# Hybrid decoder layer, feed-forward part: two norms placed later, accumulators folded by two row blocks, one subtraction on two engines, half of the last gamma products on GpSimd

## The chip, the cores and the metric

One core of a Trainium2 chip runs the whole layer as one program. The metric is the device time of one execution in microseconds (us); lower is better. TensorE is called PE here, VectorE DVE, ScalarE ACT, GpSimd POOL; SP is the engine whose queue issues nearly all transfers.

## What is computed

The layer has three parallel token mixers, a post-norm, and a squared-ReLU feed-forward with a second post-norm. The mixers are not touched by the change. What matters here, with S = 1024 tokens, a model width of 1024, a hidden width of 4096 and everything in float32:

```python
    h = layer_norm(alpha * h + mix, ln1_g, ln1_b)
    ff = jnp.square(jax.nn.relu(h @ w_up)) @ w_down
    h = layer_norm(alpha * h + ff, ln2_g, ln2_b)

def layer_norm(x, g, b):
    mu = jnp.mean(x, axis=-1, keepdims=True)
    xc = x - mu
    var = jnp.mean(xc * xc, axis=-1, keepdims=True)
    return xc * lax.rsqrt(var + LN_EPS) * g + b
```

## The kernel before, in words

**Arithmetic.** Every float32 operand of a product is split into a high part (a copy to the type fp32r, on ACT, line 76) and a low part (the difference, on DVE or POOL, line 77); a product is three PE passes, high by high, high by low, low by high (line 61). So each weight tile `W` and each operand tile `BT` or `MG` reaches PE by a transfer, a copy on ACT and a subtraction on POOL or DVE. Most of the feed-forward is computed by a block scheme with seven products in place of eight: sums and differences of 512-wide blocks are multiplied, and the seven results are added up.

**First norm.** The last part of the mixers ends with the projection `w_o`, done in two halves of 512 tokens. For the second half four row blocks n = 0 to 3 are normalised by `layer_norm` (two of them with ACT and POOL sharing the work, two, n = 2 and 3, on DVE alone but for one small power on POOL, line 1181), stored to `d_h1`, and a `flip_h1` for each is put on a list: it transposes the block and builds the split operands `xs[3]` to `xs[7]` from it on DVE, ACT and POOL, in a buffer of the ring of four that the weights use too (`W`).

**Up projection.** The first EARLY = 10 of 16 pairs are begun by `first_two`, which needs only the operands that are there already; flips 0 to 3 are taken from the list after the pairs 1, 3, 5 and 7. `c11` is the sum of two products (line 296), followed by the activation on ACT and a store. Then the 16 pairs are finished.

**Down projection.** `down(c, j, w)` is product j (1 to 7) of step c (0 to 6): four row blocks b of 512 columns go to PSUM (8 banks in rings of 3, 3 and 2, tiles `pz`, `ps`, `pt`) and are added on DVE to the SBUF accumulator `pa[j]`, 128 x 4 x 512. `pa[1]` and `pa[2]` share a tile of the ring `X`, `pa[4]` and `pa[0]` the other; `pa[5]` and `pa[3]` share a tile of the ring `O`, `pa[7]` and `pa[6]` the other. In step 0 the accumulators 2, 3 and 5 start from the rows of `h`, loaded from `d_h1`; `pa[3] -= pa[5]` (line 1058, on POOL) must come before product 5 is added to `pa[5]` (line 1070, DVE). In step 6 the products come in the order 1, 7, 3, 6, 2, 5, 4, and between them whole accumulators of 128 x 2048 are folded into each other on DVE (line 296): 6 += 1, 7 += 6, 6 += 5, 5 += 7, 4 += 7, 3 += 6, 2 += 1. After that `pa[2]` and `pa[3]` hold the two column halves of rows 0 to 3, `pa[4]` and `pa[5]` those of rows 4 to 7.

**Last rows.** The last two pairs are multiplied directly: `last_rows` computes for row blocks 4 and 5 together, then 6, 7, 0, 1, 2, 3 one by one, two PSUM tiles of 512 columns, adds each to its accumulator on DVE, takes the statistics (line 1147), and `norm_rows` does the second norm: mean and variance (1205, 1206) on DVE, a power on POOL (1207), four small operations on DVE (1208 to 1211), the scaling of each half on ACT (1213), times gamma on DVE (1214), plus beta on POOL (1215; on DVE for the last row), and the store of each half.

**Who sets the order.** A scheduler turns the program into one instruction list per engine, from the order in which it is written and an estimate of what each engine does; on the chip each engine takes its own list strictly in order, and waits where an operand isn't there. So where code stands decides only in part where its instructions stand.

Of the kernel before, what the change touches and what calls it, by code (L numbers as in the profile page):

```python
# [12 lines left out]
ALU = mybir.AluOpType  # L13
# [12 lines left out]
LN_EPS = 1e-5  # L26
# [9 lines left out]
def hybrid_layer(ctx: ExitStack, tc: tile.TileContext, a: dict, out: bass.AP):  # L36
    nc = tc.nc
# [16 lines left out]
    def const(name, shape, dt=F32):  # L54
        return sb.tile(shape, dt, tag="c_" + name, name=name, bufs=1)
# [78 lines left out]
    mhalf = const("mhalf", [P, 8])  # L134
# [15 lines left out]
    d_h1 = dr.tile([8, P, 1024], F32, name="d_h1")  # L150
# [144 lines left out]
    def add(o, a_, b_, op=ALU.add):  # L295
        nc.vector.tensor_tensor(out=o, in0=a_, in1=b_, op=op)  # L296
# [462 lines left out]
    for hf in range(NH):  # L759
# [42 lines left out]
        v = keep()  # L802
# [7 lines left out]
        for h in range(8):  # L810
# [9 lines left out]
            if h % 2 == 0 and h < 6:  # L820
                v = zv(h // 2 + 1)()
# [32 lines left out]
        lng, lnb = ln_consts(nc, st, a["ln1_g"], a["ln1_b"])  # L854
        bn = [sb.tile([P, 4, 6], F32, tag="bn", name=nm("bn"), bufs=8) for _ in range(4)]
# [21 lines left out]
        def flip_h1(n, rb, hf=hf):  # L877
# [33 lines left out]
            nc.vector.tensor_tensor(out=b21, in0=b21, in1=b22, op=ALU.subtract)  # L911
            part(4, b21, nc.vector)

        if hf == 1:
            xs[1] = (nx[0][:, 0:4], nx[1][:, 0:4])
            xs[2] = (nx[0][:, 4:8], nx[1][:, 4:8])
            operand_tiles()
        for n in range(4):
            rb = r[n // 2][:, n % 2, :]
            layer_norm(nc, small, rb, bn[n][:, 0:2, :], lng, lnb, 4.0 * LN_EPS, mhalf, None, hf == 0 or n < 2)  # L920
            nc.sync.dma_start(d_h1[4 * hf + n], rb)
            deferred.append(lambda n=n, rb=rb: flip_h1(n, rb))

    def psum(k):
# [6 lines left out]
    def first_two(i):  # L931
        w1 = halves(load_raw(a["w_up"][2 * i]), nc.gpsimd)
        o = pt("z")
        prod(o, w1, 0, 1)
        s1 = snap(o)
        nc.sync.dma_start(d_p1[i], s1)
        d = pt("s")
        prod(d, w1, 1, 2)
        c11 = st("G", [P, TH])
        add(c11, d, s1)  # L940
        act2(c11)
        nc.sync.dma_start(d_ff[i, 1], c11)

    for i in range(EARLY):
        first_two(i)
        if i % 2 and i < 8:
            deferred.pop(0)()

# [68 lines left out]
    pa = {}  # L1017

    def acc_pair(tag, i, j):
        t = st(tag, [P, 2, 4, TH])  # L1020
        pa[i], pa[j] = t[:, 0], t[:, 1]
# [3 lines left out]
    def rows_h1(j, h, f_):  # L1025
        nc.sync.dma_start(pa[j], d_h1v[:, 4 * h:4 * h + 4, f_, :])
# [22 lines left out]
    def down(c, j, wsrc):  # L1049
        f, w = operands(c, j, wsrc)  # L1050
        if c == 0 and j == 1:
            acc_pair("X", 1, 2)
            rows_h1(2, 0, 0)
            acc_pair("O", 5, 3)
            rows_h1(5, 1, 1)
            rows_h1(3, 0, 1)
            acc_pair("O", 7, 6)
            nc.gpsimd.tensor_tensor(out=pa[3], in0=pa[3], in1=pa[5], op=ALU.subtract)
        if c == 0 and j == 4:
            acc_pair("X", 4, 0)  # L1060
            rows_h1(0, 1, 0)
        for b in range(4):
            o = psum(turn[0] + b)
            bs = slice(b * P, (b + 1) * P)
            for jj in range(2):
                mm(o, f[:, 0, jj, bs], w[:, 0, jj, :], jj == 0, False)
                mm(o, f[:, 0, jj, bs], w[:, 1, jj, :], False, False)
                mm(o, f[:, 1, jj, bs], w[:, 0, jj, :], False, jj == 1)
            if c == 0 and j in (2, 3, 5):
                nc.vector.scalar_tensor_tensor(out=pa[j][:, b, :], in0=pa[j][:, b, :], scalar=ALPHA, in1=o,  # L1070
                                               op0=ALU.mult, op1=ALU.add)
            elif c == 0:
                nc.scalar.copy(pa[j][:, b, :], o)
            else:
                add(pa[j][:, b, :], pa[j][:, b, :], o)

    for c in range(NC - 1):
        m0, m1 = wd_raw(c)
        b11, b12, b21, b22 = m0[:, :, 0], m0[:, :, 1], m1[:, :, 0], m1[:, :, 1]
        down(c, 1, b11)  # L1080
        add(b11, b12, b11, ALU.subtract)
        if c < NC - 2:
            down(c, 2, b21)
            down(c, 5, b11)
            add(b12, b22, b12, ALU.subtract)
            down(c, 3, b22)
            down(c, 7, b12)
            add(b22, b22, b11, ALU.subtract)
            down(c, 6, b22)
            add(b21, b21, b22, ALU.subtract)  # L1090
            down(c, 4, b21)
            if c == 1:
                nc.vector.scalar_tensor_tensor(out=pa[4], in0=pa[0], scalar=ALPHA, in1=pa[4], op0=ALU.mult,
                                               op1=ALU.add)
            continue
        add(b12, b22, b12, ALU.subtract)
        down(c, 7, b12)
        down(c, 3, b22)
        add(b22, b22, b11, ALU.subtract)
        down(c, 6, b22)  # L1100
        add(pa[6], pa[6], pa[1])
        add(pa[7], pa[7], pa[6])
        down(c, 2, b21)
        add(b21, b21, b22, ALU.subtract)
        down(c, 5, b11)
        add(pa[6], pa[6], pa[5])
        add(pa[5], pa[5], pa[7])
        down(c, 4, b21)
        add(pa[4], pa[4], pa[7])

    lng, lnb = ln_consts(nc, st, a["ln2_g"], a["ln2_b"])
    ffs, wds = [], []
    for j in range(2):
        for m in range(2):
            i = NFF - 2 + j
# [4 lines left out]
            split(f[:, 0], f[:, 1], raw.rearrange("p h t -> p (h t)"), nc.gpsimd)  # L1120
            ffs.append(f)
            wds.append(weight(a["w_down"][2 * i + m], nc.vector if m else nc.gpsimd))
    add(pa[3], pa[3], pa[6])
    add(pa[2], pa[2], pa[1])
    def last_rows(bs):
        oo = {}
        for b in bs:
# [22 lines left out]
                      lambda cs, v, b=b: nc.sync.dma_start(outv[b][:, cs], v), b == 3)  # L1150

    last_rows((4, 5))
    for b in (6, 7, 0, 1, 2, 3):
        last_rows((b,))


def rsqrt(nc, small, v, scale, eps, mhalf, n):
# [10 lines left out]
def ln_consts(nc, st, g, b):  # L1168
    res = []
    for v in (g, b):  # L1170
        t = st("S", [P, D])
        nc.scalar.dma_start(t, bass.AP(tensor=v.tensor, offset=v.offset, ap=[[0, P], [1, D]]))
        res.append(t)
    return res


def layer_norm(nc, small, x, bn, g, b, eps, mhalf, store=None, spread=False):
    mv, e, y, z = small(2), small(1), small(1), small(1)
    nc.vector.bn_aggr(out=mv, in_=bn)
    nc.vector.tensor_scalar(out=e, in0=mv[:, 1:2], scalar1=eps, scalar2=None, op0=ALU.add)  # L1180
    nc.gpsimd.tensor_tensor(out=y, in0=e, in1=mhalf[:, :1], op=ALU.pow)
    if isinstance(x, list):
        parts = x
        for v, cs in parts:
            nc.vector.scalar_tensor_tensor(out=v, in0=v, scalar=mv[:, 0:1], in1=g[:, cs], op0=ALU.subtract,
                                           op1=ALU.mult)
    else:
        parts = [(x[:, c * 512:(c + 1) * 512], slice(c * 512, (c + 1) * 512)) for c in range(2)]
        nc.vector.scalar_tensor_tensor(out=x, in0=x, scalar=mv[:, 0:1], in1=g, op0=ALU.subtract, op1=ALU.mult)
    nc.vector.scalar_tensor_tensor(out=z, in0=y, scalar=e, in1=y, op0=ALU.mult, op1=ALU.mult)  # L1190
    nc.vector.tensor_scalar(out=z, in0=z, scalar1=-0.5, scalar2=1.5, op0=ALU.mult, op1=ALU.add)
    nc.vector.tensor_tensor(out=y, in0=y, in1=z, op=ALU.mult)
    for v, cs in parts:
        if spread:
            nc.scalar.activation(v, v, AF.Copy, scale=y)
            nc.gpsimd.tensor_tensor(out=v, in0=v, in1=b[:, cs], op=ALU.add)
        else:
            nc.vector.scalar_tensor_tensor(out=v, in0=v, scalar=y, in1=b[:, cs], op0=ALU.mult, op1=ALU.add)
        if store:
            store(cs, v)  # L1200


def norm_rows(nc, small, parts, bn, g, b, eps, mhalf, store, last):
    mv, e, y, z, nb = small(2), small(1), small(1), small(1), small(1)
    nc.vector.bn_aggr(out=mv, in_=bn)
    nc.vector.tensor_scalar(out=e, in0=mv[:, 1:2], scalar1=eps, scalar2=None, op0=ALU.add)
    nc.gpsimd.tensor_tensor(out=y, in0=e, in1=mhalf[:, :1], op=ALU.pow)
    nc.vector.scalar_tensor_tensor(out=z, in0=y, scalar=e, in1=y, op0=ALU.mult, op1=ALU.mult)
    nc.vector.tensor_scalar(out=z, in0=z, scalar1=-0.5, scalar2=1.5, op0=ALU.mult, op1=ALU.add)
    nc.vector.tensor_tensor(out=y, in0=y, in1=z, op=ALU.mult)  # L1210
    nc.vector.scalar_tensor_tensor(out=nb, in0=mv[:, 0:1], scalar=-1.0, in1=y, op0=ALU.mult, op1=ALU.mult)
    for v, cs in parts:
        nc.scalar.activation(v, v, AF.Identity, scale=y, bias=nb)
        nc.vector.tensor_tensor(out=v, in0=v, in1=g[:, cs], op=ALU.mult)  # L1214
        (nc.vector if last else nc.gpsimd).tensor_tensor(out=v, in0=v, in1=b[:, cs], op=ALU.add)  # L1215
        store(cs, v)

# [77 lines left out]
```

## Time and profile before

| what | us |
|---|---|
| median of 3 runs (lowest, highest) | 2167.03 (2166.65, 2169.42) |
| the profiled execution, its own time | 2166.51 |
| its span, first to last instruction | 2164.7 |
| PE busy | 2054.9 (95%) |
| DVE busy | 1252.5 (58%) |
| POOL busy | 959.3 (44%) |
| ACT busy | 837.7 (39%) |

All sums of the prediction are made against the profiled execution. Its time stands 1.8 us above its span, and 0.5 us below the median. The busy shares are means over the whole program; the stages that the change touches are the first begun pairs (from about 1484 us on), the first down step (from about 1807 us) and the end (from about 2078 us).

### The profile page before, as it was taken

How to read it: one execution, taken by the hardware profiler on the slowest of the kernel's cores; microseconds unless marked ns; L12 is line 12 of the kernel's file. 1: busy time of each engine (PE TensorE's matmuls, PEld its weight loads, DVE VectorE, ACT ScalarE, POOL GpSimd, SP SyncE). 2: the span in 40 equal slices, each digit the busy share in tenths (PEclk: the TensorE clock that was granted, in tenths of full speed). 3: DMA queues.
4: the chain of work that ended last, by engine and by line, in shares of the span. 5: the costliest groups of instructions: out<-in, count | busy, mean ns of one | idle time of the engine just before them, and what ended most of it. 6: DMA issues, size and time to landing. Idle time of an engine off the chain costs nothing. (4 is left out here: it accounts for less than half of the span.)

```text
span 2164.7 us, 26923 instructions
## 1 busy us (share of the span) xinstructions
PE 2054.9 (95%) x10050; PEld 1688.5 (78%) x10050; DVE 1252.5 (58%) x2092; ACT 837.7 (39%) x1480; POOL 959.3 (44%) x478
## 2 busy tenths in 40 slices
PE   8969998999999999999999999999899999999996
PEld 8747776777787898877778889887678887788875
DVE  5643276566536346256753624626566656598898
ACT  5423222344335233335433614333544454433322
POOL 2556665421222522751122242274533334777674
PEclk9989999999999999999999999999999999999998
DMA  8653432422233323544123332354657547744322
GB/s 281 215 161 127 155 121 93 145 89 69 60 102 110 124 84 117 177 145 136 59 69 103 102 123 84 121 187 144 199 186 228 182 145 240 275 136 154 116 88 78
DMA packets 125762, 299.30 MB, mean 138 GB/s; under 512 B 11408, under 2 KB 24896, under 8 KB 125632
## 3 DMA queue, kind: packets, MB, share of 16 engines
q1 hardware_dynamic: 124736, 294.42, 41.7%
q10 hardware_dynamic: 896, 3.16, 0.5%
q8 instruction: 79, 1.29, 0.3%
q14 instruction: 51, 0.42, 0.1%
HBM read 232.51 MB, written 65.03 MB: 137 GB/s over the span
## 5 line engine op out<-in xcount | busy, mean ns | idle before, releaser
L77 POOL TENSOR_TENSOR W<-R,W 128x1024 fp32r<-128x1024 f32 x205 | 497.0, 2426 | 879.3 <-ACT W L76 835.1
L61 PE MATMUL pz<-X,W 128*128 128x512 f32 x2016 | 491.9, 398 | 30.5 <-ACT W L76 11.3
L76 ACT CAST W<-R 128x1024 fp32r<-128x1024 f32 (+1 forms) x287 | 293.8, 1024 | 469.5 <-PE pz L61 226.1
L61 PEld LDWEIGHTS pz<-X,W 128*128 128x128 f32 x2016 | 377.7, 191 | 114.4 <-POOL W L77 12.9
L61 PE MATMUL pz<-O,W 128*128 128x512 f32 x1152 | 267.1, 391 | 0.0
L61 PEld LDWEIGHTS pz<-O,W 128*128 128x128 f32 x1152 | 214.9, 188 | 46.2 <-issue 1.5
L61 PE MATMUL pt<-O,W 128*128 128x512 f32 x768 | 188.0, 393 | 2.3 <-DVE T L296 2.3
L61 PEld LDWEIGHTS pt<-O,W 128*128 128x128 f32 x768 | 142.3, 188 | 39.5 <-DVE T L296 10.3
L77 DVE TENSOR_TENSOR W<-R,W 128x1024 fp32r<-128x1024 f32 (+1 forms) x84 | 100.5, 1197 | 75.3 <-ACT W L76 74.9
L61 PE MATMUL pz<-BT,W 128*128 128x512 f32 x384 | 102.1, 419 | 24.8 <-DVE G L315 9.7
L61 PEld LDWEIGHTS pz<-BT,W 128*128 128x128 f32 x384 | 76.4, 203 | 47.6 <-issue 12.7
L61 PE MATMUL ps<-W,BT 128*128 128x512 f32 x360 | 98.4, 391 | 5.3 <-DVE X L296 3.3
L61 PE MATMUL pz<-W,BT 128*128 128x512 f32 x354 | 96.3, 390 | 0.4 <-DVE X L1070 0.4
L61 PE MATMUL pz<-W,X 128*128 128x256 f32 x768 | 95.8, 284 | 0.0
L77 POOL TENSOR_TENSOR BT<-R,BT 128x1024 fp32r<-128x1024 f32 x27 | 72.1, 2671 | 51.4 <-ACT BT L76 51.4
L61 PE MATMUL ps<-X,W 128*128 128x512 f32 x384 | 93.0, 391 | 1.6 <-DVE G L296 1.6
L61 PEld LDWEIGHTS pz<-W,X 128*128 128x128 f32 x768 | 93.1, 192 | 0.0
L61 PE MATMUL ps<-T,W 128*128 128x512 f32 x384 | 92.2, 389 | 0.0
L61 PEld LDWEIGHTS ps<-X,W 128*128 128x128 f32 x384 | 72.6, 189 | 17.5 <-DVE G L296 2.3
L341 POOL TENSOR_TENSOR R<-R,R 128x512 f32<-128x512 f32 x48 | 64.3, 1340 | 48.8 <-DMA R<-in_w_gate_dram 31.1
L61 PEld LDWEIGHTS ps<-T,W 128*128 128x128 f32 x384 | 72.1, 188 | 15.0
L77 POOL TENSOR_TENSOR MG<-R,MG 128x1024 fp32r<-128x1024 f32 (+1 forms) x30 | 79.5, 2651 | 9.0 <-ACT MG L76 9.0
(277 smaller groups left out, 3454.9 us busy)
## 6 DMA issues: line engine op xcount, KB each, us to landing
R<-d_ff SPq DMA_DIRECT2D x49, 512.0 KB, 3.6
R<-in_w_b_dram SPq DMA_DIRECT2D x48, 512.0 KB, 3.5
R<-in_w_up_dram SPq DMA_DIRECT2D x42, 512.0 KB, 4.1
R<-in_w_gate_dram SPq DMA_DIRECT2D x40, 512.0 KB, 3.6
d_ff<-T SPq DMA_DIRECT2D x56, 256.0 KB, 2.8
d_z<-T SPq DMA_DIRECT2D x52, 256.0 KB, 2.0
G<-d_z SPq DMA_DIRECT2D x48, 256.0 KB, 2.8
d_ff<-S SPq DMA_DIRECT2D x48, 256.0 KB, 2.3
```

The source lines that it names most:

```text
L61: nc.tensor.matmul(o, lhsT=l, rhs=r, start=start, stop=stop, skip_group_check=more)
L76: (hi_copy or nc.scalar.copy)(hi, src)
L77: (lo_eng or nc.gpsimd).tensor_tensor(out=lo, in0=src, in1=f32(hi), op=ALU.subtract)
L341: nc.gpsimd.tensor_tensor(out=o, in0=a_, in1=b_, op=op)
```

## The change

It has four parts. In the first norm, the norms of row blocks 2 and 3 of the second half are written after the begun pairs 2 and 4 instead of ahead of pair 0. In the first down step, the subtraction `pa[3] -= pa[5]` is done half on DVE and half on POOL, and stands ahead of the allocation of the next pair of accumulators. In the last down step the folds are done for two row blocks at a time (128 x 1024), 14 operations for 7, some of them written later. In the second norm, the product with gamma of the second half of every row but the last is on POOL, where the additions of beta are already.

```diff
+        norms = []
         for n in range(4):
             rb = r[n // 2][:, n % 2, :]
-            layer_norm(nc, small, rb, bn[n][:, 0:2, :], lng, lnb, 4.0 * LN_EPS, mhalf, None, hf == 0 or n < 2)
-            nc.sync.dma_start(d_h1[4 * hf + n], rb)
+
+            def norm(n=n, rb=rb, hf=hf, bn=bn[n], gb=(lng, lnb)):
+                layer_norm(nc, small, rb, bn[:, 0:2, :], *gb, 4.0 * LN_EPS, mhalf, None, hf == 0 or n < 2)
+                nc.sync.dma_start(d_h1[4 * hf + n], rb)
+
+            if hf == 0 or n < 2:
+                norm()
+            else:
+                norms.append(norm)
             deferred.append(lambda n=n, rb=rb: flip_h1(n, rb))
...
     for i in range(EARLY):
         first_two(i)
+        if i in (2, 4):
+            norms.pop(0)()
         if i % 2 and i < 8:
             deferred.pop(0)()
...
             rows_h1(3, 0, 1)
+            for e, eng in enumerate((nc.vector, nc.gpsimd)):
+                bb = slice(2 * e, 2 * e + 2)
+                eng.tensor_tensor(out=pa[3][:, bb, :], in0=pa[3][:, bb, :], in1=pa[5][:, bb, :], op=ALU.subtract)
             acc_pair("O", 7, 6)
-            nc.gpsimd.tensor_tensor(out=pa[3], in0=pa[3], in1=pa[5], op=ALU.subtract)
...
+    def merge(h, *terms):
+        bb = slice(2 * h, 2 * h + 2)
+        for i, j in terms:
+            add(pa[i][:, bb, :], pa[i][:, bb, :], pa[j][:, bb, :])
...
         down(c, 6, b22)
-        add(pa[6], pa[6], pa[1])
-        add(pa[7], pa[7], pa[6])
         down(c, 2, b21)
         add(b21, b21, b22, ALU.subtract)
+        merge(0, (6, 1), (7, 6))
         down(c, 5, b11)
-        add(pa[6], pa[6], pa[5])
-        add(pa[5], pa[5], pa[7])
+        merge(1, (6, 1), (7, 6))
         down(c, 4, b21)
-        add(pa[4], pa[4], pa[7])
+        merge(0, (6, 5), (5, 7), (4, 7))
...
-    add(pa[3], pa[3], pa[6])
-    add(pa[2], pa[2], pa[1])
...
     last_rows((4, 5))
+    merge(1, (6, 5), (5, 7), (4, 7))
     for b in (6, 7, 0, 1, 2, 3):
         last_rows((b,))
+        if b >= 6:
+            merge(b - 6, (3, 6), (2, 1))
...
         nc.scalar.activation(v, v, AF.Identity, scale=y, bias=nb)
-        nc.vector.tensor_tensor(out=v, in0=v, in1=g[:, cs], op=ALU.mult)
+        (nc.vector if last or cs.start == 0 else nc.gpsimd).tensor_tensor(out=v, in0=v, in1=g[:, cs], op=ALU.mult)
         (nc.vector if last else nc.gpsimd).tensor_tensor(out=v, in0=v, in1=b[:, cs], op=ALU.add)
```

Three places of the instruction lists. The lines of `norm_rows` are 17 higher in the changed kernel: 1224 is the power, 1225 to 1228 are the four small operations, 1230 is ACT's scaling, 1231 gamma, 1232 beta. The tiles named `sm` hold one number per row.

First, DVE at the norms of row blocks 2 and 3 (T_11218 holds both, S the constants; G<-ps,G is c11 of pair 0, and W_11639 or W_11611 the buffer of flip 0). Before:

```order
L1190 SCALAR_TENSOR_TENSOR sm_11536<-sm_11535,sm_11534 128x1
L1179 BN_AGGR sm_11547<-bn_11228 128x2
L296 TENSOR_TENSOR G_11595<-ps_11582,G_11579 128x512
L1191 TENSOR_SCALAR sm_11536<-sm_11536 128x1
L1180 TENSOR_SCALAR sm_11548<-sm_11547 128x1
L1189 SCALAR_TENSOR_TENSOR T_11218<-T_11218,sm_11547,S_11221 128x1024
...
L1198 SCALAR_TENSOR_TENSOR T_11218<-T_11218,sm_11549,S_11223 128x512 x2
L296 TENSOR_TENSOR G_11634<-ps_11621,G_11618 128x512
L905 TENSOR_TENSOR W_11639<-W_11639 128x512
```

With the change:

```order
L296 TENSOR_TENSOR G_11567<-ps_11554,G_11551 128x512
L1207 SCALAR_TENSOR_TENSOR sm_11681<-sm_11680,sm_11679 128x1
L1196 BN_AGGR sm_11798<-bn_11228 128x2
L1208 TENSOR_SCALAR sm_11681<-sm_11681 128x1
L1197 TENSOR_SCALAR sm_11799<-sm_11798 128x1
L1206 SCALAR_TENSOR_TENSOR T_11218<-T_11218,sm_11798,S_11221 128x1024
...
L1215 SCALAR_TENSOR_TENSOR T_11218<-T_11218,sm_11800,S_11223 128x512 x2
L296 TENSOR_TENSOR G_11606<-ps_11593,G_11590 128x512
L905 TENSOR_TENSOR W_11611<-W_11611 128x512
```

c11 of pair 0 has moved up by two small rows; both norms still stand ahead of the first row of flip 0 (L905). In SP's list, the store of row block 2 now stands behind two stores of begun pairs, and that of block 3 behind four.

Second, POOL in the last rows, from the power of row 6 to the power of row 7 and a little further. Before:

```order
L1207 TENSOR_TENSOR sm_16210<-sm_16209,mhalf 128x1
L1215 TENSOR_TENSOR X_14257<-X_14257,S_16027 128x512
L1215 TENSOR_TENSOR O_14008<-O_14008,S_16027 128x512
L1207 TENSOR_TENSOR sm_16261<-sm_16260,mhalf 128x1
L1215 TENSOR_TENSOR X_14257<-X_14257,S_16027 128x512
L1215 TENSOR_TENSOR O_14008<-O_14008,S_16027 128x512
L1207 TENSOR_TENSOR sm_16312<-sm_16311,mhalf 128x1
```

With the change:

```order
L1224 TENSOR_TENSOR sm_16214<-sm_16213,mhalf 128x1
L1231 TENSOR_TENSOR O_14008<-O_14008,S_16028 128x512
L1232 TENSOR_TENSOR X_14258<-X_14258,S_16030 128x512
L1232 TENSOR_TENSOR O_14008<-O_14008,S_16030 128x512
L1231 TENSOR_TENSOR O_14008<-O_14008,S_16028 128x512
L1232 TENSOR_TENSOR X_14258<-X_14258,S_16030 128x512
L1232 TENSOR_TENSOR O_14008<-O_14008,S_16030 128x512
L1224 TENSOR_TENSOR sm_16267<-sm_16266,mhalf 128x1
L1232 TENSOR_TENSOR X_14258<-X_14258,S_16030 128x512
L1231 TENSOR_TENSOR O_14008<-O_14008,S_16028 128x512
L1232 TENSOR_TENSOR O_14008<-O_14008,S_16030 128x512
L1224 TENSOR_TENSOR sm_16320<-sm_16319,mhalf 128x1
```

Before, the power of row 7 stands behind the two additions of row 5, and the power of row 0 behind those of row 6. Now the power of row 7 stands behind the three operations of row 5 and the three of row 6, and from there on every power stands behind the three operations of the row just before it.

Third, DVE of the changed kernel in the last rows: the four small operations of row 7 (sm_16268 to sm_16269) with what stands between them, down to row 7's product with gamma.

```order
L1225 SCALAR_TENSOR_TENSOR sm_16268<-sm_16267,sm_16266 128x1
L296 TENSOR_TENSOR X_14006<-X_14006,ps_16287 128x512
L1226 TENSOR_SCALAR sm_16268<-sm_16268 128x1
L1161 BN_STATS bn_16313<-X_14006 128x6
L1227 TENSOR_TENSOR sm_16267<-sm_16267,sm_16268 128x1
L1228 SCALAR_TENSOR_TENSOR sm_16269<-sm_16265,sm_16267 128x1
L1231 TENSOR_TENSOR X_14258<-X_14258,S_16028 128x512
```

Two 512-wide operations of row 0 stand between row 7's small ones. For row 0 it is the same; for rows 1 and 2 the four small operations stand together, and the 512-wide ones (two for row 1, one for row 2) behind them, ahead of gamma.

## Rows read from the trace of the kernel before

**Rows 1.** Stretches: length, busy us (and count) of PE, PEld, DVE, ACT, POOL, granted clock, DMA.

```profile
1844.00:1849.00 5.00, 5.00 (x13) 3.89 (x13) 2.72 (x5) 1.45 (x2) 5.00 (x3) 0.50 0.58 208
...
2101.00:2105.00 4.00, 3.80 (x10) 3.02 (x11) 4.00 (x3) 0.00 (x0) 4.00 (x2) 0.59 0.00 0
...
2112.00:2145.00 33.00, 33.00 (x147) 27.10 (x145) 31.05 (x71) 7.62 (x10) 18.11 (x16) 1.00 0.21 79
2145.00:2165.00 20.00, 0.14 (x1) 0.00 (x0) 12.10 (x30) 4.55 (x6) 6.50 (x6) 0.61 0.22 81
```

**Rows 2.** Timeline, begun pairs: start, us, engine, line, out<-in [idle before <-releaser].

```profile
1496.83 0.63 DVE L296 TENSOR_TENSOR G<-ps,G 128x512 f32<-128x512 f32 x1
...
1497.50 2.70 DVE L1189 SCALAR_TENSOR_TENSOR T<-T,sm,S 128x1024 f32<-128x1024 f32 x1
...
1504.36 1.42 DVE L1198 SCALAR_TENSOR_TENSOR T<-T,sm,S 128x512 f32<-128x512 f32 x2
...
1513.13 1.04 ACT L76 CAST W<-R 128x1024 fp32r<-128x1024 f32 x1 [1.71 <-DVE T L77]
...
1514.23 0.93 PE L61 MATMUL pz<-X,W 128*128 128x512 f32 x2 [4.53 <-ACT W L76]
```

**Rows 3.** Timeline, first down step and the start of the second.

```profile
1837.79 4.53 POOL L1058 TENSOR_TENSOR O<-O 128x2048 f32<-128x2048 f32 x1 [8.84 <-DMA O<-d_h]
...
1842.69 2.38 POOL L77 TENSOR_TENSOR BT<-R,BT 128x1024 fp32r<-128x1024 f32 x1 [0.37 <-ACT BT L76]
...
1843.70 2.93 PE L61 MATMUL ps<-W,MG 128*128 128x512 f32 x6 [4.34 <-DVE O L1070]
...
1853.22 1.22 DVE L296 TENSOR_TENSOR T<-T 128x1024 f32<-128x1024 f32 x1
...
1872.94 3.39 DVE L296 TENSOR_TENSOR T<-T,T 128x1024 f32<-128x1024 f32 x1 [3.93 <-POOL W L77]
...
1876.99 1.66 PE L61 MATMUL pt<-W,MG 128*128 128x512 f32 x6 [0.54 <-DVE X L296]
```

**Rows 4.** Timeline, folds of the last down step and the first last row.

```profile
2080.33 2.29 DVE L296 TENSOR_TENSOR O<-O,X 128x2048 f32<-128x2048 f32 x1
...
2096.05 4.49 DVE L296 TENSOR_TENSOR O<-O,O 128x2048 f32<-128x2048 f32 x1
...
2101.20 1.25 PE L61 MATMUL ps<-W,BT 128*128 128x512 f32 x3 [3.27 <-DVE X L296]
...
2112.57 0.68 DVE L296 TENSOR_TENSOR X<-X,ps 128x512 f32<-128x512 f32 x1
```

**Rows 5.** The chain that ended last, rows 1 and 2: start, us, engine, tile, line.

```profile
2143.66 0.56 POOL sm L1207
2144.25 0.22 DVE sm L1208
...
2145.55 0.82 ACT X L1213
2146.39 0.69 DVE X L1214
...
2150.27 0.56 POOL sm L1207
```

**Rows 6.** Timeline, last rows: a small operation and five of POOL's.

```profile
2121.80 1.25 DVE L1208 SCALAR_TENSOR_TENSOR sm<-sm,sm 128x1 f32<-128x1 f32 x1
...
2125.01 0.55 POOL L1207 TENSOR_TENSOR sm<-sm,mhalf 128x1 f32<-128x1 f32 x1 [0.73 <-DVE sm L1206]
...
2130.85 0.55 POOL L1207 TENSOR_TENSOR sm<-sm,mhalf 128x1 f32<-128x1 f32 x1 [0.82 <-DVE sm L1206]
...
2142.29 1.28 POOL L1215 TENSOR_TENSOR O<-O,S 128x512 f32<-128x512 f32 x1
...
2147.16 1.26 POOL L1215 TENSOR_TENSOR X<-X,S 128x512 f32<-128x512 f32 x1 [2.95 <-DVE X L1214]
...
2156.70 0.55 POOL L1207 TENSOR_TENSOR sm<-sm,mhalf 128x1 f32<-128x1 f32 x1
```

## The prediction

> **What bounds the kernel now.** I read first the busy times: PE is busy 95% of the span, so a change of work on another engine counts only where PE waits for it, or behind PE's last matmul. Then the timeline at the four edited places, with PE's waits: after flip 0 it waits 4.53 us for a copy on ACT [rows 2], in the first down step 4.34 us for an evicting addition on DVE [rows 3], at the last folds 3.27 us [rows 4]. Each is followed by some 5 us in which the granted clock is 0.50 to 0.59 [rows 1], the lower of PE's two levels (1.2 of 2.4 GHz), so such a wait costs half of the next 4 to 5 us besides, 2 to 2.5 us; the wait of 0.54 us [rows 3] is priced at its own length. Last the windows and the chain of the end: from 2112 us PE and DVE are both nearly full (33.00 and 31.05 of 33 us, POOL 18.11), from 2145 us PE is done and 20 us follow without it [rows 1]. In them the chain goes round through three engines: power on POOL, four small operations on DVE, scaling on ACT, gamma on DVE, and the next row's power [rows 5]. So three of the four parts must shorten a wait of PE to count, and the fourth works on the chain of the end itself.
>
> **Part 1, the norms.** The lists show that both norms still stand on DVE ahead of flip 0. What moves is c11 of pair 0: 0.63 us, two small rows earlier. Before it ends at 1497.46, and the subtraction of the mean behind it, which is held by POOL, takes until 1500.20 [rows 2]; the addition now lies in that held time or just ahead of it. The norm of row block 3 ends at 1505.78, flip 0 follows, ACT's copy comes at 1513.13 when flip 0 has given its buffer back, and PE's 4.53 us wait ends on that copy [rows 2]. None of these loses an operation ahead of it. The two stores that SP issues now stand behind two and four stores of c11; nothing reads those rows before the second down step's stage some 300 us later, and the queue carries no load that PE waits for at this place. I take **0**, ends -0.7 and +0.7 us: the one addition, either way.
>
> **Part 2, the subtraction.** Before: 4.53 us on POOL. After: 128 x 1024 on DVE at 1.22 us, and as much on POOL at 2.38 us [rows 3], 3.6 us if they exclude each other. That they do is seen in two rows: the same kind of 128 x 2048 fold takes 2.29 us alone and 4.49 us beside POOL [rows 4], and a one-column operation 1.25 us beside POOL [rows 6] against 0.22 us [rows 5]. The Trainium skill, "SBUF — State Buffer", section "Who interferes with whom", says the same as a rule: VectorE and GpSimd share an exclusive port lock, and the one that starts first holds it for its whole instruction; by it the halves take 3.6 us, without it 2.38 us side by side, and the rows here agree with the rule.
> PE waits at 1843.70 because product 5's evictions wait for this subtraction. With DVE's half first, PE could resume near 1840.2, 0.9 us after it stopped. Then product 7's low part is next: POOL makes it at 1842.69 and takes 2.38 us [rows 3], so PE waits for it until 1845.1, about 1.65 us. With POOL's half first it resumes near 1842.5, 1.2 us sooner. Local gain: 1.2 us at the least, and at the most 4.34 + 2.5 (the clock) - 0.9 - 1.65 = 4.3 us. But POOL has a queue ahead of it in the second step, which doesn't move by what PE gains: at 1872.94 a DVE fold has waited 3.93 us for POOL, and the addition behind it gates PE at 1876.99 [rows 3]. A PE that comes there 4 us sooner waits there 4 us longer, with a drop of the clock. What is kept is about 0.6 to 1.2 us at best, and a drop there costs up to 1.9 us net. I take **0**, ends -1.2 and +1.9.
>
> **Part 3, the folds.** 14 operations of 128 x 1024 at 1.22 us [rows 3] are 17.1 us, 7 of 128 x 2048 at 2.29 us [rows 4] 16.0: +1.1 us of DVE. In return an eviction waits behind a shorter piece. PE's wait of 3.27 us at 2101.20 [rows 4] and the 4 us at clock 0.59 behind it [rows 1] (1.6 us lost) can shrink, so PE may end some 2 to 3 us earlier. But the last rows are paced by DVE's and POOL's turns: the folds, moved behind row 6 in the program, still stand in DVE's list ahead of row 4's first addition, so this comes at about 2112.6 as before [rows 4], and PE's gain ends in full PSUM tiles. I take **0**, ends -2.0 (the wait's clock drop gone and kept, with a little of the wait) and +1.1.
>
> **Part 4, gamma of half rows.** Seven multiplications of 128 x 512 leave DVE (0.69 us [rows 5]), and seven come to POOL, which has no multiplication of this size in the trace. The nearest rows are its additions of the same shape, 1.28 and 1.26 us [rows 6]: I take 1.27; the DVE rate (0.69) is the lower bound, POOL's 2.38 us for twice the columns [rows 3] confirms the upper. What counts is the queue that they join. Every power stands on POOL too, and from row 7 on it now stands behind three operations of the row just before it, the first of which needs that row's gamma chain. One turn from power to power then is:
> power to scaling, 2145.55 - 2143.66 = 1.89, less the one 512-wide operation between the small ones (0.63 to 0.68): 1.25; scaling to gamma, 2146.39 - 2145.55 = 0.84; gamma to POOL, 2147.16 - 2146.39 = 0.77 [rows 5, 6]; three operations, 3.81. Sum 6.67 us.
> For rows 7 and 0 two operations of 0.65 stand between the small ones: 7.97 each. For row 1 two stand behind them, beside ACT's 0.84: 7.13. For row 2 one, hidden: 6.67. Together 29.7 us from row 7's power to row 3's. Before it was 2156.70 - 2130.85 = 25.85 [rows 6]: **+3.9**. From row 6's power to row 7's, six operations and the power are at least 0.55 + 6 x 1.27 = 8.17, against 5.84 before [rows 6]: +2.3, and with two small operations held by POOL (1.03 more each) +4.3; I take **+2.5**. Behind row 3's power nothing changes, since the last row is all on DVE. Part 4 is **+6.4 us**; ends +3.1 (2.3, and 6.67 for each turn: +0.8) and +10.3 (4.3, and 3.9 with one small operation held in each of rows 7 and 0). The 7 x 0.69 = 4.8 us that DVE saves don't lie on this chain beyond what is counted.
>
> **Sum.** 2166.51 + 0 + 0 + 0 + 6.4 = 2172.9 us for an execution like the profiled one; the median stands 0.5 us above that: **2173.4 us**. A measurement of this kernel tells about 0.2% (4.3 us) from no change.
>
> **The rivals.**
> A is the forecast: the loop through POOL sets the end.
> B, **faster**: the end is bound by DVE. For it: DVE is busy 31.05 of 33 us from 2112 to 2145, POOL only 18.11 [rows 1]. Then what counts is 7 x 0.69 = 4.8 us off DVE: 2167.0 - 4.8 = 2162.2. It decides when the turn from power to power stays below 25.85 / 4 = 6.46 us, that is, when powers don't wait for POOL's own queue. Against it: my shortest turn is 6.67, and the power is in the chain of the end [rows 5]. The Trainium skill, "Perfetto Trace Analysis", section "Optimizing Scalar/DVE Operations", has it so: with DVE saturated, work may go to ScalarE or even GpSimd, though the same place warns that GpSimd shares DVE's port; the trace agrees on the warning [rows 4].
> C, **partly offset**: part 4 as forecast, but PE's wait at 1843.70 goes with its clock drop and the gain of 4.3 us is kept, as POOL's queue of the second step moves up too, or part 3 keeps its 2 us and more: 2173.4 - 4.3 = 2169.1, within 0.2%. For it: with its clock [rows 1] that wait costs 4.34 + 2.5 = 6.8 us, more than the gain that is asked. Against: the 3.93 us for POOL at 1872.94 [rows 3].
> D, **worse**: the wait moves to 1876.99 with a clock drop (+1.9), and small operations are held by POOL in more turns (+2.5): 2177.8.
> That part 1 does not do what it says (the lists keep the norms where they were) is in every case's sum.
>
> **How the numbers follow.** A 0.62, C 0.20, B 0.10, D 0.08: 2173.4 is A's. A's own range, by the ends of part 4, is 2170.1 to 2177.3. The range for 8 in 10 leaves out B, most of D and some of A's and C's ends: 2166.5 to 2177.0. Slower by over 0.2% means above 2171.4: most of A (0.56) and D, 0.64. Within 0.2%: the rest of A's lower end and C, 0.25. Faster: B and a little of C, 0.11.
>
> **What would show it.** Right: the powers of rows 7 and 3 some 29 to 30 us apart, those of rows 6 and 7 more than 8, each with a wait for POOL's own queue; three POOL operations of about 1.27 us per row; the first addition of the last rows near 2112.6; PE's last matmul not later than before, and yet a later end; the wait near 1514 still 4.5 us; the halves of the subtraction one after the other; fold rows near 1.2 us, and a shorter wait near 2100 without a low clock. Wrong: a shorter span, powers that follow each other in under 6.5 us, a POOL multiplication far from 1.27 us, or an end that already stands several us earlier than before at the first last-row addition.

## The result, and the profile after

The changed kernel takes 2176.93 us (median of 4 runs, 2175.72 to 2179.31) where the kernel before takes 2166.84 (4 runs). The ratio is 1.0052, with a 95% interval of 1.0038 to 1.0066: **+11.3 us** (8.2 to 14.3), slower. A second comparison, below, gives 1.0042 (1.0030 to 1.0054), +9.1 us. The direction was forecast; the forecast was +6.4 us, and the excess is what has to be explained. The profiled execution has its own time at 2179.31 us and a span of 2177.5.

Windows of the changed kernel, with the columns of [rows 1]: the second down step's start, the last folds, and the two stretches of the end.

```profile
1879.00:1884.00 5.00, 5.00 (x12) 3.98 (x13) 5.00 (x4) 0.32 (x1) 4.78 (x2) 0.50 0.21 79
...
2105.00:2109.00 4.00, 3.96 (x17) 3.30 (x18) 4.00 (x4) 0.09 (x1) 1.01 (x1) 1.00 0.01 2
2118.00:2147.00 29.00, 29.00 (x130) 24.01 (x129) 22.43 (x50) 6.10 (x8) 16.63 (x16) 1.00 0.17 63
2147.00:2178.00 31.00, 0.78 (x4) 0.32 (x2) 15.93 (x41) 6.07 (x8) 14.45 (x14) 0.57 0.20 77
```

DVE is no longer full in the last rows (22.43 of 29 us; before, 31.05 of 33), and what follows PE's last matmul has grown from 19.6 to 29.7 us (it ended at 2145.14 before and ends at 2147.78 now). Near 2105 us the clock stays at 1.00, where it was 0.59 [rows 1]; near 1879 us it is 0.50, where the 5 us behind PE's wait ran at 1.00 before.

POOL's timeline from the power of row 6 to that of row 0, and the last power (L1224 powers, L1231 gamma, L1232 beta):

```profile
2129.99 1.01 POOL L1224 TENSOR_TENSOR sm<-sm,mhalf 128x1 f32<-128x1 f32 x1
2130.98 1.28 POOL L1231 TENSOR_TENSOR O<-O,S 128x512 f32<-128x512 f32 x1
2132.22 1.28 POOL L1232 TENSOR_TENSOR X<-X,S 128x512 f32<-128x512 f32 x1
2133.47 1.29 POOL L1232 TENSOR_TENSOR O<-O,S 128x512 f32<-128x512 f32 x1
2136.41 1.29 POOL L1231 TENSOR_TENSOR O<-O,S 128x512 f32<-128x512 f32 x1 [1.65 <-ACT O L1230]
2137.64 1.30 POOL L1232 TENSOR_TENSOR X<-X,S 128x512 f32<-128x512 f32 x1
2138.89 1.29 POOL L1232 TENSOR_TENSOR O<-O,S 128x512 f32<-128x512 f32 x1
2140.13 0.56 POOL L1224 TENSOR_TENSOR sm<-sm,mhalf 128x1 f32<-128x1 f32 x1
2144.19 1.29 POOL L1232 TENSOR_TENSOR X<-X,S 128x512 f32<-128x512 f32 x1 [3.49 <-DVE X L1231]
2145.43 1.29 POOL L1231 TENSOR_TENSOR O<-O,S 128x512 f32<-128x512 f32 x1
2146.80 1.28 POOL L1232 TENSOR_TENSOR O<-O,S 128x512 f32<-128x512 f32 x1
2148.04 0.55 POOL L1224 TENSOR_TENSOR sm<-sm,mhalf 128x1 f32<-128x1 f32 x1
...
2169.49 0.55 POOL L1224 TENSOR_TENSOR sm<-sm,mhalf 128x1 f32<-128x1 f32 x1
```

A multiplication takes as long as an addition (1.28 and 1.29 us). Row 6's power to row 7's is 10.14 us (5.84 before, [rows 6]), row 7's to row 3's 29.36 (25.85). In the chain that ended last (start, us, engine, tile, line) gamma on POOL now stands in the way of the power:

```profile
2143.41 0.70 DVE X L1231
2144.12 0.07 issue
2144.19 1.29 POOL X L1232
2145.47 1.26 POOL O L1231
2146.73 0.07 issue
2146.80 1.28 POOL O L1232
2148.08 0.52 POOL sm L1224
```

What made the step from row 6 to row 7 that long is DVE's timeline of row 6's small operations: two of them take over 1.2 us, where such operations take about 0.2 alone (0.22 [rows 5]). Each starts 0.06 to 0.09 us after one of POOL's operations above and ends with it.

```profile
2131.04 1.24 DVE L1225 SCALAR_TENSOR_TENSOR sm<-sm,sm 128x1 f32<-128x1 f32 x1 [0.44 <-POOL sm L1224]
...
2133.56 1.21 DVE L1228 SCALAR_TENSOR_TENSOR sm<-sm,sm 128x1 f32<-128x1 f32 x1
```

The timeline of the first and second down step (L1069 is the split subtraction):

```profile
1839.49 1.23 DVE L1069 TENSOR_TENSOR O<-O 128x1024 f32<-128x1024 f32 x1 [0.55 <-DMA O<-d_h]
1839.54 3.44 POOL L1069 TENSOR_TENSOR O<-O 128x1024 f32<-128x1024 f32 x1 [8.14 <-DMA O<-d_h]
...
1842.17 1.65 PE L61 MATMUL ps<-W,MG 128*128 128x512 f32 x6 [0.36 <-DVE O L1082]
...
1847.29 1.19 PE L61 MATMUL pz<-W,BT 128*128 128x512 f32 x4 [1.65 <-POOL BT L77]
...
1874.88 3.36 DVE L296 TENSOR_TENSOR T<-T,T 128x1024 f32<-128x1024 f32 x1 [7.11 <-POOL W L77]
...
1878.89 2.93 PE L61 MATMUL pt<-W,MG 128*128 128x512 f32 x6 [3.69 <-DVE X L296]
```

The halves exclude each other: POOL's, started 0.05 us after DVE's, takes 3.44 us. PE's wait of 4.34 us [rows 3] and the low clock behind it [rows 1] are gone, 0.36 and 1.65 us are left. But the wait at 1876.99, 0.54 us before, is 3.69 us now, with the low clock behind it.

Last the folds (timeline of PE and DVE) and the wait after flip 0:

```profile
2105.04 0.96 PE L61 MATMUL ps<-W,BT 128*128 128x512 f32 x3 [2.29 <-DVE X L296]
...
2117.90 0.68 DVE L296 TENSOR_TENSOR X<-X,ps 128x512 f32<-128x512 f32 x1
```

```profile
1514.89 1.04 ACT L76 CAST W<-R 128x1024 fp32r<-128x1024 f32 x1 [1.70 <-DVE T L77]
...
1515.99 1.04 PE L61 MATMUL pz<-X,W 128*128 128x512 f32 x2 [4.53 <-ACT W L76]
```

PE's wait at the folds is 1 us shorter, and still the first addition of the last rows comes 5.3 us later than in [rows 4]: 2.4 us of it were there in this execution at 1814 us already, and 2.9 us come between there and the last rows (2.0 ahead of the folds, 0.9 in their stretch). The wait after flip 0 is the same 4.53 us.

### The profile page after: what moved, and what is told of

It reads as the page before. It is cut to its first block, busy times and chain, and to the rows that moved or that the text cites. A ratio compares the mean times of both kernels' runs of the same rounds, so it can differ in the third digit from the quotient of the medians.

```text
span 2177.5 us, 26930 instructions
## 1 busy us (share of the span) xinstructions
PE 2055.2 (94%) x10050; PEld 1688.6 (78%) x10050; DVE 1256.0 (58%) x2093; ACT 836.8 (38%) x1480; POOL 961.2 (44%) x485
## 3 DMA queue, kind: packets, MB, share of 16 engines
q8 instruction: 79, 1.29, 0.2%
## 5 line engine op out<-in xcount | busy, mean ns | idle before, releaser
L76 ACT CAST W<-R 128x1024 fp32r<-128x1024 f32 (+1 forms) x287 | 293.7, 1024 | 469.6 <-PE pz L61 226.0
L77 POOL TENSOR_TENSOR MG<-R,MG 128x1024 fp32r<-128x1024 f32 (+1 forms) x30 | 77.1, 2570 | 14.3 <-ACT MG L76 14.3
## 6 DMA issues: line engine op xcount, KB each, us to landing
d_ff<-T SPq DMA_DIRECT2D x56, 256.0 KB, 2.8
d_z<-T SPq DMA_DIRECT2D x52, 256.0 KB, 2.0
G<-d_z SPq DMA_DIRECT2D x48, 256.0 KB, 2.9
d_ff<-S SPq DMA_DIRECT2D x48, 256.0 KB, 2.3
```

The lines of the kernel that those rows point to most:

```text
L76: (hi_copy or nc.scalar.copy)(hi, src)
L77: (lo_eng or nc.gpsimd).tensor_tensor(out=lo, in0=src, in1=f32(hi), op=ALU.subtract)
```

## Experiments

Two stretches of each profiled execution are compared. **A**: PE's wait of 0.78 to 0.79 us near 1814 us (the start of the first down step) to the first addition of the last rows; before 298.56, changed 301.45 us. **B**: that addition to the end of the span; before 52.13, changed 59.60 us. B repeats within 0.15 us between kernels with the same last rows, so it says more than the time; A does not (see below). Every kernel was timed in five rounds beside the kernel before; "us" behind a ratio is the ratio's excess times 2166.

**The parts, one at a time.** Gamma alone:

```diff
-        nc.vector.tensor_tensor(out=v, in0=v, in1=g[:, cs], op=ALU.mult)
+        (nc.vector if last or cs.start == 0 else nc.gpsimd).tensor_tensor(out=v, in0=v, in1=g[:, cs], op=ALU.mult)
```

> The kernel before with the gamma change alone. Theory 1 (POOL's queue: in the last rows every power waits for the three operations of the row before it): about +7.5 us on the kernel before, with row 6's power to row 7's near 10 us instead of 5.84, and row 7's to row 3's near 29.4 instead of 25.85. Rival 1 (gamma on POOL costs only because the folds changed DVE's turn as well): under +4 us here. Rival 2 (the last rows are bound by DVE, which loses 4.8 us of work): faster than before.

Ratio 1.0028 (1.0018 to 1.0037), +6.1 us. B is 59.18, +7.05 us; row 6's power to row 7's 10.00 us, row 7's to row 3's 28.21. Rivals 1 and 2 fall. Theory 1 holds so far, though row 7's to row 3's is 1.2 us shorter than it said.

The changed kernel with that line put back:

> The changed kernel with the product with gamma of every half row back on DVE. Theory 1: the 7.5 us of the last rows go, and what is left over the kernel before is the stall that moved to the second down step (+2.0) and the folds (+0.9): about +2.9 us on the kernel before. Rival 1 (the parts depend on each other): +6 us or more is left. If the change in the first down step is only chance: about +0.9.

1.0008 (0.9997 to 1.0019), +1.7 us; B is 52.08. Rival 1 falls; +2.9 and +0.9 us can't be told apart by this time. So gamma is worth 7.05 us in B on the kernel before and 7.5 us on top of the other parts, and 0.0034 of the ratio (7.4 us) against the second run of the changed kernel:

> The changed kernel once more, against the same runs of the kernel before as its neighbours. Theory 1 (POOL's queue in the last rows +7.5, the folds +0.9, the rest a matter of the single execution): +7 to +9.5 us. Rival (the first step and the norms cost something of their own on top): +10 us or more.

1.0042 (1.0030 to 1.0054), +9.1 us; A 300.31, B 59.65. The interval leaves Theory 1 and the rival both open.

The subtraction alone (on DVE and POOL, as in the change):

> The kernel before with the subtraction on two engines alone. Theory 1 (the wait of PE moves from near 1844 us to near 1877 us, because POOL's queue there does not come earlier, and takes the drop of the clock with it): +1.5 to +2.5 us, with a wait of 3 to 4 us near 1877 and about 5 us at a granted clock of 0.5 behind it. Rival 3 (the gain at the first stall is kept): -3 to -4.5 us. Rival 4 (nothing follows): within 0.7 us.

1.0004 (0.9993 to 1.0015), +0.9 us; A 298.69. PE waits 1.72 us near 1848 and 1.88 us at 1878.22, with a clock of 0.66 in the 5 us behind it. Rival 3 falls; Theory 1's wait is there but shorter, and the time can't tell it from rival 4. The change without the split:

> The changed kernel with the subtraction of residuals whole on POOL again. Theory 1 (the split only decides where PE waits): +7.5 to +9.5 us on the kernel before, as the changed kernel, at most 2 us below it. Rival (the split with the wait that it moves costs 2 us and more of its own): 2 us or more below the changed kernel's +9.1 to +11.3.

1.0033 (1.0022 to 1.0045), +7.1 us, 2 us below the changed kernel's second comparison, with intervals that overlap; A 300.12, B 59.70. The traces say more. PE's wait near 1875 us, in the seven executions with the split and the second step as it was: 1.88 to 3.69 us, the clock behind it 0.50 or 0.66 each time. In the seven without the split: 0.53 to 2.80 us, the clock 1.00 in six of them, 0.50 in one (gamma alone, 2.80 us). So the split makes that wait likely, and is not needed for it. What the wait costs shows in the first piece of A, from PE's wait near 1814 us to DVE's operation on `T` near 2070 us, ahead of every fold: 257.64 to 257.98 us in the six of the fourteen with a wait of 2.80 us or more there and a clock of 0.50 behind it, 255.01 to 256.86 us in the other eight, about 2 us apart. By the split alone the fourteen are not parted: 255.79 to 257.98 us with it (mean 257.3), 255.01 to 257.94 without (mean 256.0). Its 1.3 us are an estimate from these means, not shown.

The folds alone:

> The kernel before with the folds by two row blocks alone. Theory 1: +0.9 us (the first addition of the last rows comes 0.9 us later, as 14 operations of 1.2 us and more stand ahead of it instead of 7, and PE's shorter wait near 2101 us does not matter). Rival 5 (the shorter wait of PE and the clock that stays up are kept): -1.5 us or better.

1.0007 (0.9997 to 1.0018), +1.5 us; B 52.03. From DVE's operation on `T` near 2070 us to the first addition of the last rows it is 42.89 us before, 43.81 in the changed kernel and 44.11 here: 0.9 to 1.2 us more, whatever PE gained at its shorter wait. Over all the traces it is 43.69 to 44.21 us in nine with the folds (mean 43.9) and 42.87 to 42.95 in nine without: about 1.0 us, clear of the scatter. DVE is busy for 43.55 of the 43.81 us in the changed kernel, for 41.27 of 42.89 before. Rival 5 falls.

B hides that the folds move the turns inside it. POOL's timeline of this kernel, with gamma still on DVE, the powers of rows 6, 7 and 3 (L1212):

```profile
2122.72 0.55 POOL L1212 TENSOR_TENSOR sm<-sm,mhalf 128x1 f32<-128x1 f32 x1 [0.83 <-DVE sm L1211]
...
2127.03 0.55 POOL L1212 TENSOR_TENSOR sm<-sm,mhalf 128x1 f32<-128x1 f32 x1 [0.41 <-DVE sm L1211]
...
2154.51 0.54 POOL L1212 TENSOR_TENSOR sm<-sm,mhalf 128x1 f32<-128x1 f32 x1
```

Row 6's power to row 7's is 4.31 us here (5.84 before), row 7's to row 3's 27.48 (25.85).

The norms alone:

> The kernel before with the two norms written after begun pairs alone. Theory 1 (the lists hardly change, both norms still stand ahead of flip 0): within 1 us of the kernel before, PE's wait after flip 0 still 4.5 us. Rival (the later stores or the moved addition cost): +1 to +2 us, seen between PE's waits near 1514 and near 1582 us, 67.9 to 68.5 us apart in the kernel before and the changed one.

0.9994 (0.9984 to 1.0005), -1.3 us, no difference that can be told; the wait is 4.53 us again. PE's waits near 1514 and 1582 us are 66.7 to 68.9 us apart in the eight traces with the moved norms and 66.4 to 68.7 in the ten without (68.0 in the mean of both), so the rival's 1 to 2 us are not there. Theory 1 holds.

**Which rows cost.** Gamma on POOL for rows 7, 0, 1, 2 only, and for 4, 5, 6 only (the row's number is passed to `norm_rows` for it):

```diff
-(nc.vector if last or cs.start == 0 else nc.gpsimd)
+(nc.vector if last or cs.start == 0 or row in (4, 5, 6) else nc.gpsimd)
...
+(nc.vector if last or cs.start == 0 or row < 4 or row == 7 else nc.gpsimd)
```

> The changed kernel with gamma of the second half on POOL only for rows 7, 0, 1 and 2; rows 4, 5 and 6 have it on DVE again. Theory 1 (each turn waits for three operations of the row just before it): row 6's power to row 7's falls back to about 5.8 us, row 7's to row 3's is 29 to 30 us instead of 25.85; with the folds +4.5 us on the kernel before. Rival (the seven products add up, 1.25 us each or less, wherever they stand): 4/7 of the full cost in the powers from row 4 to row 3, about 4.2 us, of which a part between rows 6 and 7.

> The changed kernel with gamma of the second half on POOL only for rows 4, 5 and 6. Theory 1 (the lead that POOL's queue has in the kernel before, one row, is used up by the six operations ahead of row 7's power): row 6's power to row 7's 8.2 to 10.2 us, and row 7's to row 3's 25.5 to 27 us, since the lead is gone there too; +4 to +6.5 us on the kernel before, so that this half and the other add up to more than the whole. Rival (costs add up by the product): 3/7 of the full cost, about 3.2 us.

The late four: 1.0017 (1.0009 to 1.0026), B 54.72, +2.6 us; the powers of rows 6 and 7 4.31 us apart, those of rows 7 and 3 30.14 (with the folds alone 4.31 and 27.48). The early three: 1.0028 (1.0015 to 1.0042), B 56.45, +4.3 us; 10.15 and 26.21 us. Three products cost more than four, so a price per product is out. But the halves add up to 6.9 of 7.5 us, not to more than the whole: that part of Theory 1 falls.

**Is it POOL's count of operations?** Beta of the second half on DVE, so that POOL has two again:

```diff
-        (nc.vector if last else nc.gpsimd).tensor_tensor(out=v, in0=v, in1=b[:, cs], op=ALU.add)
+        (nc.vector if last or cs.start else nc.gpsimd).tensor_tensor(out=v, in0=v, in1=b[:, cs], op=ALU.add)
```

> The changed kernel with the second half's addition of beta on DVE: gamma of that half stays on POOL, and POOL has two operations of 512 columns per row again. Theory 1 (three operations ahead of each power are what costs): the first addition of the last rows to the end of the span falls from 59.6 us to 51 to 54. Rival (that gamma of the second half stands on POOL, with ACT before it and DVE behind it, is what costs, whatever stands there besides): 57 us or more.

1.0050 (1.0039 to 1.0061), +10.8 us; B 58.07. Theory 1 as I had put it falls, the rival holds. This kernel's timeline, from row 0's operations to row 1's power:

```profile
2145.84 1.26 POOL L1231 TENSOR_TENSOR O<-O,S 128x512 f32<-128x512 f32 x1 [3.46 <-ACT O L1230]
2147.06 1.26 POOL L1232 TENSOR_TENSOR X<-X,S 128x512 f32<-128x512 f32 x1
2147.13 1.73 DVE L1232 TENSOR_TENSOR O<-O,S 128x512 f32<-128x512 f32 x1 [1.35 <-POOL O L1231]
...
2150.41 0.55 POOL L1224 TENSOR_TENSOR sm<-sm,mhalf 128x1 f32<-128x1 f32 x1 [2.09 <-DVE sm L1223]
```

The power no longer waits in POOL's queue; it waits for DVE, and DVE has waited 1.35 us for gamma on POOL and then some 1.0 us more (1.73 for 0.69) beside POOL's next operation. In these rows it is the half row in series that costs, and POOL takes about twice DVE's time for it (1.26 us for 0.69). Each row but the last has one operation more on DVE than in the changed kernel, so the run does not part the two engines cleanly.

The opposite step, beta of rows 0 to 2 on DVE, for both halves and for the second half (condition `row < 3`, or `row in (0, 1, 2) and cs.start`, in the same line of the kernel before):

> The kernel before with the opposite step: the additions of beta of rows 0, 1 and 2 on DVE, so that POOL has only the powers there. Theory 1 (POOL's queue and the lock set the turn): row 0's power to row 3's shorter than the 21.55 us of before, and 1 to 3 us less in all. Rival 2 (the last rows are bound by DVE): six additions of 0.69 us more, +3 to +4 us.

> The kernel before with the additions of beta of the second half of rows 0, 1 and 2 on DVE, so that POOL has one operation of 512 columns and a power per row there. Theory 1 (the turn is as long as the chain of power, DVE, ACT, DVE and POOL's operations of the row): the turns of rows 1 to 2 and 2 to 3 shrink from 6.61 and 6.43 us to 5.2 to 6.1. Rival 2 (bound by DVE): no shorter, and +1 to +2 us in all.

1.0006 (0.9997 to 1.0015) and 1.0001 (0.9992 to 1.0011); B 53.33 and 53.22. No gain, and no loss of the size of rival 2: the turn from row 1 to row 2 shrinks (2.88 and 5.78 us for 6.61), but that from row 0 to row 1 grows (10.65 and 10.55 for 8.51), and in the first kernel that from row 2 to row 3 too (9.16 for 6.43): DVE's list there has row 0's beta ahead of row 1's statistics. Row 0's power to row 3's is 22.69 and 22.58 us for 21.55, so Theory 1's shorter stretch did not come either. POOL's timeline of that kernel, from row 1's power to row 3's, shows each power waiting for DVE:

```profile
2144.89 0.55 POOL L1207 TENSOR_TENSOR sm<-sm,mhalf 128x1 f32<-128x1 f32 x1 [5.18 <-DVE sm L1206]
2147.77 0.55 POOL L1207 TENSOR_TENSOR sm<-sm,mhalf 128x1 f32<-128x1 f32 x1 [2.34 <-DVE sm L1206]
2156.93 0.55 POOL L1207 TENSOR_TENSOR sm<-sm,mhalf 128x1 f32<-128x1 f32 x1 [8.61 <-DVE sm L1206]
```

So in these runs taking load off either engine did not shorten the last rows; the traces show a chain over both, whose order counts.

**Where the gain of the split goes.** DVE's operation at 1874.88 (the subtraction `b22 -= b11`, which the prediction calls a fold) waits until POOL has read `b22` for product 3's low part. That part on DVE, with and without the split:

```diff
-        split(w[:, 0], w[:, 1], wsrc, nc.vector if turn[0] % 2 else nc.gpsimd)
+        split(w[:, 0], w[:, 1], wsrc, nc.vector if turn[0] % 2 or (c, j) == (1, 3) else nc.gpsimd)
```

> The kernel before with the subtraction on two engines, and in the second down step the low part of product 3's weights on DVE instead of POOL, which takes away what the fold near 1875 us waits for. Theory 1 (what the split gains near 1844 us is lost in the second step, where DVE waits for POOL): now it is kept, -2 to -5 us on the kernel before, no wait of PE over 1 us near 1877 us and the granted clock 1.0 behind it. Rival (the gain is lost elsewhere, in the transfers or PSUM): within 1 us.

> The kernel before with the low part of product 3's weights in the second down step on DVE alone, the subtraction as before. Theory 1 (the wait near 1877 us is there in the executions in which PE came early, with or without the split): -0.5 to -2.5 us, from the executions of the kernel before that had a wait and a low clock there; PE's wait near 1844 us with its clock stays. Rival: no difference to the version with the split, so that the split gains nothing.

> The kernel with the low part of product 3's weights in the second down step on DVE, once more. Theory 1: -1 to -3.5 us on the kernel before, and no wait of PE near 1877 us. Rival (the first measurement was chance): within 0.5 us.

With the split 0.9992 (0.9983 to 1.0001), A 295.54; without it 0.9989 (0.9976 to 1.0001) and, again, 0.9979 (0.9970 to 0.9988), A 295.25 and 295.32. The wait near 1877 us is gone, and A is 3.2 us shorter than in the profiled execution of the kernel before. But the split adds nothing, and the 2 to 5 us that Theory 1 gave for both together are not reached by the middle of the interval (-1.7 us). PE's timeline with the split:

```profile
1844.31 0.73 PE L61 MATMUL pz<-W,BT 128*128 128x512 f32 x2 [0.30 <-ACT BT L76]
...
1846.75 1.19 PE L61 MATMUL pz<-W,BT 128*128 128x512 f32 x4 [1.71 <-POOL BT L77]
...
1864.03 1.20 PE L61 MATMUL pz<-W,MG 128*128 128x512 f32 x4 [0.66 <-POOL MG L77]
...
1881.56 1.62 PE L61 MATMUL pz<-W,BT 128*128 128x512 f32 x6 [1.35 <-DVE X L296]
```

Four waits of 4.0 us in sum at full clock. In the second run without the split there is one:

```profile
1841.15 2.93 PE L61 MATMUL ps<-W,MG 128*128 128x512 f32 x6 [2.97 <-DVE O L1070]
```

The windows behind it and near 1877 us, with the columns of [rows 1]:

```profile
1841.15:1846.15 5.00, 5.00 (x16) 4.01 (x17) 3.52 (x6) 2.86 (x4) 4.90 (x3) 0.69 0.87 346
1874.00:1880.00 6.00, 6.00 (x27) 4.65 (x26) 6.00 (x8) 2.57 (x3) 5.96 (x3) 1.00 0.53 165
```

2.97 us, and 5 us at a clock of 0.69, 1.55 us lost: 4.5 us, and nothing near 1877. So the rival holds: PE that comes sooner only waits for the next thing. The version with the low part on DVE alone, with medians near 2162 us, is the one here that beats both kernels; of its two intervals, the second is clear of no change. With the folds added to it:

> That kernel with the folds by two row blocks added. Theory 1 (the folds cost 0.5 to 0.9 us where PE's wait behind them is not what bounds): 0.5 to 0.9 us above the same kernel without the folds. Rival (the folds gain once PE comes without a wait from the second step): below it.

0.9993 (0.9984 to 1.0003), 3 us above the second run without them (0.9979) by the ratios; A 298.06. The rival falls. Of the 2.74 us that A is longer, 0.85 lie in the stretch of the folds, as elsewhere, and 1.89 ahead of them, where PE's wait in the first step was 3.73 us in this execution; whether the folds have a part in that stays open.

## Why the prediction was wrong in size and right in direction

The sum now: 7.5 us (gamma), 1.0 (folds), 1.3 (the split, an estimate that the times do not show), 0 (norms): 9.8 us, between the two measurements of 9.1 and 11.3. The step that failed is part 4's +2.5 us between the powers of rows 6 and 7, which measured +4.3; next to it stand the zeros of parts 2 and 3. By its own steps:

- **Part 1, 0:** right. Norms alone can't be told from no change, and the wait of 4.53 us is the same.
- **Part 2, 0 (ends -1.2 and +1.9):** its working came as written: halves in series, a wait of 1.65 us for POOL's low part, and then the wait at 1876.99, grown. But I took the middle, and set the drop of the clock there aside as rival D at 0.08, although every step of the working led to it. It was there in all seven executions with the split and the second step as it was.
- **Part 3, 0 (ends -2.0 and +1.1):** the shorter wait and the kept clock came, and gained nothing, as said. But the +1.1 of more DVE work, put at nothing, did not vanish: the first addition comes about 1.0 us later, as DVE, not PE, sets it. That the size fits is in part luck: the working has every fold at its time alone, and six of the fourteen took 2.19 to 2.83 us for 1.22 (before, three of seven 3.85 to 4.49 us for 2.29).
- **Part 4, +6.4:** 7.5 measured. The turns were right: 7.97, 7.97, 7.13, 6.67 forecast, 7.91, 7.81, 6.82, 6.82 measured, with three operations on POOL ahead of each power. The term that failed is the +2.5 between the powers of rows 6 and 7: +4.3, the upper end, as two of row 6's small operations took 1.24 and 1.21 us beside POOL's. Gamma of the early three rows gives that step by itself (10.15 us, 4.31 without them). Up to row 6's power 0.35 us was gained back.
- **Parts 3 and 4 added as if apart:** both steps of part 4 are counted from the turns of the kernel before, and the folds alone change those (4.31 and 27.48 us for 5.84 and 25.85). On top of the folds gamma costs 5.8 us from row 6 to row 7 and 1.9 in the turns. The sum is nearly the same only because the folds alone leave B as it was (52.03 us).
- **"The loop through POOL"** as the cause is too narrow. With one operation less on POOL the last rows are 1.5 us shorter, and still 6 us longer than before: in that run the power waits on DVE, which waits for gamma on POOL.
- **The range** ended at 2177.0, below D's own 2177.8. The ratio of the first comparison, on the 2167.03 that the forecast started from, gives 2178.3 us, above it; the second gives 2176.1, inside. They differ by less than either interval is wide. Whichever holds, three terms came out at or near their upper ends, and I had let them vary one at a time, though nothing in the working lets one exclude another.

Rival B fell: with gamma off DVE, DVE stood idle (22.43 of 29 us) and waited. Rival C fell: the gain at 1843.70 was not kept. Of the signs, the first addition near 2112.6 us and a last matmul not later than before did not come (2117.90, and 2147.78 for 2145.14); 2.4 us of both were there at 1814 us already.

## What to carry over

In a tail that goes round through several engines, count what stands in each queue between one link of the chain and the next, before counting the load of an engine: 4.8 us off a DVE that was 94% busy bought nothing, and one operation of 1.28 us more per row on POOL, between a row's scaling and the next row's power, cost 7.5. Where the working of a step ends in a wait that moves, price the moved wait, its clock included, and not zero. Where several terms have an upper end and none excludes another, let the range take these ends together. And where two parts of a change touch the same stretch, take the times that the second is counted from with the first in place.

## What the runs showed that I had not expected

A wait's length alone does not tell whether PE's clock falls behind it. The same 12 matmuls, in PE's timeline near 1205 us, before (first) and in the changed kernel, far ahead of every edit:

```profile
1205.20 1.69 PE L61 MATMUL ps<-W,T 128*128 128x256 f32 x12 [2.37 <-DVE O L99]
```

```profile
1205.49 2.84 PE L61 MATMUL ps<-W,T 128*128 128x256 f32 x12 [2.30 <-DVE O L99]
```

After 2.37 us the granted clock is 1.00, after 2.30 us 0.57 in the same 4 us, and the stretch to the wait near 1237 us is 1.5 us longer. In the first down step waits of 1.65 us (the changed kernel) and 1.71 (the split with the low part on DVE) were followed by 4 us at a clock of 1.00, waits of 1.72 (the split alone) and 1.71 (gamma of the early three) by 4 us at 0.57. So the prediction's price of such a wait holds for the execution it was read from. Single executions of the kernel before lay between 2161 and 2173 us here; how much of that comes from such places is not shown, nor is what decides between the two outcomes. That scatter is why an edit of 1 or 2 us is read from a stretch of the trace rather than from the time.
